# Attention halves added from PSUM, the last keys' low parts behind the first maxima, half of a scaling on ScalarE

## The chip, the cores and the metric

The kernel runs on one core of a Trainium2 chip (trn2), one launch per execution. The metric is the device time of an execution in microseconds. A profiled execution also has a span, from its first to its last instruction. The engines are TensorE (PE, with its weight loads as PEld), VectorE (DVE), ScalarE (ACT), GpSimd (POOL) and SyncE (SP, which issues the DMAs).

## The reference

One layer of a residual block over 1024 tokens of width 1024, in float32:

```python
h = rmsnorm(x, norm_mix)
proj = h @ w_in                          # 3384 columns, split between two groups of heads
o_a = sparse_attention(qa, ka, va, ...)  # 8 heads of 64; an indexer keeps 256 keys per query
o_b = gla(qb, kb, vb, ...)               # 4 heads, a recurrence over 16 chunks of 64 tokens
x = x + concat(o_a, o_b) @ w_out
h = rmsnorm(x, norm_ffn)
x = x + (silu(h @ w_ffn_gate) * (h @ w_ffn_up)) @ w_ffn_down   # width 2816
return rmsnorm(x, norm_final)
```

The attention's softmax runs over the kept keys of chunks that are not in the query's future, with a bias by relative position. The change touches three places: the copy of the projected keys, the end of the attention's product with the values, and the multiplication of the normed tokens by norm_ffn.

## The kernel before, in words

**Two parts of a number.** Matmuls run in a rounded format (fp32r). Operands are therefore split into a high part, a rounded copy made by ACT, and a low part, the difference made by DVE or POOL, and a product is the sum of three matmuls (high x high, high x low, low x high). Every operand costs an ACT copy and a subtraction.

**The order is planned.** The program does not write its instructions in a fixed order. Generators (threads) ask for an engine with a price in ns (`yield DVE, dve(256)`), for a slot of a pool, or for an event, and the class `Flow` runs them against a clock of its own; at each step it emits the instruction that could start first by its prices, and of those within 20 ns the one with the lower rank. What comes out is a fixed sequence for each engine. An event has no counterpart on the chip: it only sets where an instruction comes in its engine's sequence. Slots stand for memory: `ps` four PSUM banks of 512 columns, `pl` two double banks, `hp` seven half pages, `kb` six quarter tiles, `pg` pages. `give` returns a slot, at the planner's time.

**The keys (L1240 to 1259).** The last projection writes the keys, 128 rows (two heads) by 512 tokens to a bank. `evac_ka(hf, c, b)` copies each head's 64 rows to the high half of the key tile on ACT (L1251), writes the low part to the other 64 rows on DVE (L1257), and returns the bank. `c` is the pair of heads, 0 to 3, `hf` the half of the tokens; for c = 3 both banks are complete at the end of the projection.

**The attention.** Tokens are taken in pairs of tiles p (256 tokens), in the order 1, 2, 3, 0, and in each pair 8 heads. `softmax(p, h, e)` writes the logits lg of one tile e to a double bank (pair 0: to a ps bank), DVE adds the mask and takes the row's extreme value mn (L1337; pair 0: L1339), ACT takes the exponential (L1343), DVE a reciprocal (L1345), POOL scales (L1347), and the event ("p", t, h) is set. `value(n, i)` transposes the probabilities on PE (L1360) to a ps bank ptr, splits them (L1372 ACT, L1375 DVE) and multiplies them by the values (L1384), whose stationary operand holds high and low parts side by side: rows 0 to 63 of the output bank `av` get the products with the high parts, rows 64 to 127 those with the low parts. Two heads share an output bank. `combine(n)` adds the two halves after each second head: ACT copies the bank to a half page (L1399), the bank is returned, a quarter tile is asked for, DVE adds rows 64 to 127 to rows 0 to 63 for either head (L1405), POOL splits the sum (L1411, L1413), and SP stores it. In pair 0 the probabilities are kept in quarter tiles as well. Behind pair 3 the output projection (`oa`, L372 to 374) is open to PE as its weights arrive and are split (L257, L262).

**The second norm.** `second_norm(j, b)` adds the residual (y, L1554 for the last tile, L1567 for the others), norms the tile, transposes it on PE to banks of four blocks (tp, L1589), and `scale_tile(j, t, d0, b)` multiplies each block by norm_ffn on its way to the tile hr (L1605), two blocks at a time, with t = 1 for the tiles 0 to 3 (the last four to be made) and 0 for the others. `sum_tile` builds sums of blocks on DVE (L1663, 1667, 1671), `blocks` further differences (L1687), and `split_b` splits each into hc (L1635 ACT, L1629 DVE). The FFN multiplies by a scheme with seven products of such sums: fa, fc and fb are its first output banks, B22 (fc) is made of the t = 1 tiles, and T2 (fb) of the sums.

Of the kernel before, what the change touches and what calls it, by code (L numbers as in the profile page):

```python
# [14 lines left out]
AF = mybir.ActivationFunctionType  # L15
# [25 lines left out]
PAIRS = [1, 2, 3, 0]  # L41
# [6 lines left out]
def f32(ap):  # L48
    return ap.bitcast(F32)


PE, ACT, DVE, POOL, DMA = range(5)


def act(n, acc=False):
    return n / 1.2 + (280 if acc else 50)


def dve(n):
    return n / 0.96 + 68  # L60


def pool1(n):
    return n * 0.836 + 160


def pool2(n):
    return n * 2.105 + 150
# [6 lines left out]
def dvf(n):  # L75
    return n / 0.96 + 155
# [249 lines left out]
def block_kernel(ctx: ExitStack, tc: tile.TileContext, a: dict, out: bass.AP, dbg=None):  # L326
    nc = tc.nc
# [16 lines left out]
    def page(shape, dt, name):  # L344
        return big.tile(shape, dt, name=name, tag="pg", bufs=NPG)
# [10 lines left out]
    def half(shape, dt, name):  # L356
        return sm.tile(shape, dt, name=name, tag="hp", bufs=NHP)

    def quarter(shape, dt, name):
        return sm.tile(shape, dt, name=name, tag="kb", bufs=NKB)  # L360
# [56 lines left out]
    nrm = cst.tile([P, 2, KT], F32, name="nrm")  # L417
# [50 lines left out]
    ev = fl.event  # L468
    pg = Slots(fl, NPG - NT - 1)
    hp, kb, ps, pl = (Slots(fl, n) for n in (NHP, NKB, 4, 2))  # L470
# [768 lines left out]
    def evac_ka(hf, c, b):  # L1239
        o = slice(hf * HB, (hf + 1) * HB)  # L1240
        if hf == 0:
            yield ev("gla")
            for e in range(2):
                yield pg
                Ks[2 * c + e] = page([P, S], F32R, "K")
            ev("ka page", c).set()
        yield ev("ka page", c)
        yield ACT, 2 * act(HB)
        for e in range(2):
            r = slice(e * 64, e * 64 + 64)  # L1250
            nc.scalar.activation(Ks[2 * c + e][r, o], b[r, :], AF.Copy)  # L1251
        yield DVE, 2 * dve(HB)
        for e in range(2):
            k = Ks[2 * c + e]
            r = slice(e * 64, e * 64 + 64)
            q = slice(64 - e * 64, 128 - e * 64)
            nc.vector.scalar_tensor_tensor(k[q, o], b[r, :], 1.0, f32(k[r, o]), op0=ALU.mult, op1=ALU.subtract)  # L1257
        ps.give()
        ev("ka", hf, c).set()
# [49 lines left out]
    PB, OP = {}, {}  # L1309
# [82 lines left out]
    def combine(n):  # L1392
        p, h = units[n]
        c = h // 2
        yield ev("av", n, p)
        yield hp
        yield ACT, act(HB)
        lo = half([P, HB], F32, "lo")
        nc.scalar.activation(lo, OP.pop((p, c)), AF.Copy)  # L1399
        ps.give()  # L1400
        yield kb
        so = quarter([P, 256], F32, "so")
        for e in range(2):
            yield DVE, dve(256)
            nc.vector.tensor_tensor(so[e * 64:(e + 1) * 64, :], lo[0:64, e * 256:(e + 1) * 256],  # L1405
                                    lo[64:128, e * 256:(e + 1) * 256], op=ALU.add)
        hp.give()
        yield hp
        yield POOL, pool1(256)
        m = half([P, 2, 256], F32R, "mxa")  # L1410
        nc.gpsimd.tensor_scalar(m[:, 0, :], so, 1.0, 1.0, op0=ALU.mult, op1=ALU.mult)  # L1411
        yield POOL, pool2(256)
        nc.gpsimd.tensor_tensor(m[:, 1, :], so, f32(m[:, 0, :]), op=ALU.subtract)  # L1413
        kb.give()
        yield DMA, 450
        nc.sync.dma_start(d_ma[p][:, :, c, :], f32(m))
        hp.give(LOAD)
        ev("mix", p, c).set(LOAD)
# [122 lines left out]
    hr, BC = {}, {}  # L1541
# [57 lines left out]
    def scale_tile(j, t, d0, b):  # L1599
        o = slice(j % 4 * P, (j % 4 + 1) * P)  # L1600
        b3 = b.rearrange("p (d n) -> p d n", n=P)
        for d in range(0, 4, 2):
            yield DVE, dvf(256)
            g = nrm[:, 1, d0 + d:d0 + d + 2]
            nc.vector.tensor_tensor(hr[(d0 + d) // 2, t][:, :, o], b3[:, d:d + 2, :],  # L1605
                                    g[:, :, None].to_broadcast([P, 2, P]), op=ALU.mult)
        ps.give()
        ev("scaled", j, d0).set()
        if t and d0:
            done_b[0] += 1  # L1610
            if done_b[0] == 4:
                for k in range(4):
                    fl.spawn(split_b("B22", k, block(1, 1, k)), 1.1 + 0.01 * k)
        if bool(d0) != bool(t):
            yield ev("scaled", j, 4 - d0)
            fl.spawn(sum_tile(j) if t else first_half(j), 1.05)

    def block(j, t, k):

        return hr[2 * j + k // 2, t][:, k % 2, :]  # L1620
# [10 lines left out]
    def split_b(name, k, src):  # L1631
        yield pg
        yield ACT, acf(HB)
        w = page([P, 2, HB], F32R, "hc")
        nc.scalar.activation(w[:, 0, :], src, AF.Copy)  # L1635
        yield from low(w[:, 1, :], src, f32(w[:, 0, :]), False)
        BC[name, k] = w
        ev("B", name, k).set()
# [632 lines left out]
    def main():  # L2271
# [18 lines left out]
        yield from proj_t(evac_va)  # L2290
        yield from proj_f(evac_qa, 1)
        yield from proj_f(evac_ka, 0)
        fl.spawn(load_attention(), 15)
        fl.spawn(softmaxes(), 16)
# [62 lines left out]
```

## Time and profile before

| | us |
|---|---|
| median of 3 runs (lowest, highest) | 1287.97 (1284.92, 1291.63) |
| the profiled execution | 1289.89 |
| its span | 1288.1 |
| PE busy | 1243.2 (97% of the span) |
| DVE busy | 933.7 (72%) |
| ACT busy | 600.6 (47%) |
| POOL busy | 394.5 (31%) |

The mean granted clock of PE is 0.985 of its full speed. A share of busy time is an average over stages: the projections run to 404 us with the indexer and the recurrence beside them, the attention to about 555 us, the output projection and the second norm to about 640 us, the FFN to the end. Matmuls are pipelined and their ends are modelled, so a busy PE is not PE at its peak.

### The profile page before, as it was taken

What the parts mean: (1) busy time and instruction counts of PE and PEld (TensorE: products, weight loads), DVE (VectorE), ACT (ScalarE), POOL (GpSimd) and SP (SyncE); (2) the same over time, 40 slices, a digit from 0 to 9 for tenths busy, and PEclk for the clock granted to TensorE, in tenths of its full rate; (3) what the DMA queues carried; (4) which work ended last, traced back from release to release, by engine and by line L of the source; (5) the groups of instructions that cost most, each with busy time, mean ns of one, the idle gap of its engine ahead of it and who ended that gap; (6) DMA issues with size and microseconds to landing.
All of it is one profiled execution on the core that took longest, in us unless ns stands there. A gap on an engine that the chain in (4) does not pass through costs nothing. (4 is left out here: it accounts for less than half of the span.)

```text
span 1288.1 us, 17923 instructions
## 1 busy us (share of the span) xinstructions
PE 1243.2 (97%) x6074; PEld 1022.6 (79%) x6074; DVE 933.7 (72%) x1739; ACT 600.6 (47%) x1113; POOL 394.5 (31%) x375
## 2 busy tenths in 40 slices
PE   6999999999999999899989999999999999999997
PEld 5878878767787998778868787878888888888885
DVE  6389988979964998843688887768778653335875
ACT  4467777634524787621344444444444332222333
POOL 5324335523401544310103334334333120000340
PEclk8999999979999999999989999999999999999999
DMA  6653221334563437683015777767665479555664
GB/s 212 191 150 123 74 74 42 131 138 152 178 221 100 114 85 201 190 270 129 34 61 184 273 245 258 254 246 261 229 219 205 133 258 379 180 196 190 225 238 164
DMA packets 124909, 232.06 MB, mean 180 GB/s; under 512 B 14297, under 2 KB 72465, under 8 KB 124817
## 3 DMA queue, kind: packets, MB, share of 16 engines
q1 hardware_dynamic: 124816, 230.91, 54.4%
q8 instruction: 48, 0.79, 0.3%
q14 instruction: 45, 0.36, 0.1%
HBM read 148.02 MB, written 82.85 MB: 179 GB/s over the span
## 5 line engine op out<-in xcount | busy, mean ns | idle before, releaser
L1626 POOL TENSOR_TENSOR w<-raw,w 128x512 fp32r<-128x512 f32 x60 | 85.3, 1424 | 214.2 <-ACT w L1766 182.3
L1766 ACT ACTIVATE w<-raw 128x512 fp32r<-128x512 f32 x132 | 81.4, 626 | 54.3 <-DMA d_wd<-wd 15.0
L760 DVE TENSOR_SCALAR_CACHE_REDUCE junk_v<-acc,thr 128x768 bf16<-128x768 f32 (+3 forms) x128 | 103.7, 810 | 2.0
L262 POOL TENSOR_TENSOR w<-st,w 128x512 fp32r<-128x512 f32 x52 | 73.4, 1422 | 75.5 <-ACT w L257 73.3
L767 ACT ACTIVATE junk_a<-acc,thr 128x1024 bf16<-128x1024 f32 x64 | 73.4, 1146 | 46.2 <-DVE thr L784 37.5
L2102 DVE TENSOR_TENSOR da<-U,da 128x512 fp32r<-128x512 f32 x54 | 43.1, 799 | 53.7 <-ACT da L2100 53.5
L2100 ACT ACTIVATE da<-U 128x512 fp32r<-128x512 f32 x54 | 33.7, 630 | 98.8 <-PE da L2156 33.2
L372 PE MATMUL pj<-w,hT 128*128 128x512 f32 x192 | 79.2, 412 | 0.0
L2031 ACT ACTIVATE wd<-wd 128x512 fp32r<-128x512 f32 x77 | 48.3, 629 | 62.1 <-DMA d_wd<-wd 28.1
L373 PE MATMUL pj<-w,hT 128*128 128x512 f32 x192 | 75.9, 395 | 0.0
L374 PE MATMUL pj<-w,hT 128*128 128x512 f32 x192 | 75.8, 395 | 0.0
L372 PE MATMUL pf<-hT,w 128*128 128x512 f32 x192 | 75.8, 395 | 0.0
L1347 POOL TENSOR_SCALAR pb<-pb,sume 128x384 f32<-128x384 f32 (+3 forms) x64 | 47.7, 751 | 89.9 <-DVE sume L1345 74.1
L374 PE MATMUL pf<-hT,w 128*128 128x512 f32 x192 | 74.8, 389 | 0.0
L373 PE MATMUL pf<-hT,w 128*128 128x512 f32 x192 | 74.8, 389 | 0.0
L1807 PE MATMUL fb<-hc,w 128*128 128x512 f32 x176 | 69.5, 395 | 3.9 <-DVE gt L1842 2.5
L1808 PE MATMUL fb<-hc,w 128*128 128x512 f32 x176 | 69.2, 393 | 3.8 <-DVE hc L1629 3.8
L1808 PE MATMUL fc<-hc,w 128*128 128x512 f32 x176 | 69.5, 395 | 2.4 <-DVE hc L1629 2.4
L1807 PE MATMUL fc<-hc,w 128*128 128x512 f32 x176 | 69.1, 392 | 0.4 <-DVE gt L1861 0.4
L2156 PE MATMUL da<-db,da 128*128 128x512 f32 x176 | 68.7, 390 | 0.7 <-DVE da L2102 0.7
L1626 POOL TENSOR_TENSOR wd<-wd 128x512 fp32r<-128x512 f32 x33 | 49.8, 1511 | 63.7 <-ACT wd L2031 55.9
L2154 PE MATMUL da<-db,da 128*128 128x512 f32 x176 | 68.6, 390 | 0.6 <-ACT da L2100 0.6
(315 smaller groups left out, 3643.7 us busy)
## 6 DMA issues: line engine op xcount, KB each, us to landing
d_wd<-wd SPq DMA_DIRECT2D x77, 512.0 KB, 3.5
db<-d_wd SPq DMA_DIRECT2D x77, 512.0 KB, 4.3
st<-w_in SPq DMA_DIRECT2D x52, 256.0 KB, 2.8
raw<-w_ffn_gate SPq DMA_DIRECT2D x22, 512.0 KB, 5.2
raw<-w_ffn_up SPq DMA_DIRECT2D x22, 512.0 KB, 4.5
wd<-w_ffn_down SPq DMA_DIRECT2D x44, 256.0 KB, 4.8
d_ux<-gt SPq DMA_DIRECT2D x9, 512.0 KB, 2.6
d_uy<-gt SPq DMA_DIRECT2D x9, 512.0 KB, 3.5
```

Source lines behind the costliest of these rows:

```text
L262: (eng or self.nc.gpsimd).tensor_tensor(w[:, 1, :], st, f32(w[:, 0, :]), op=ALU.subtract)
L372: mm(ps, lh, rh, start=first, stop=False)
L373: mm(ps, lh, rl, start=False, stop=False)
L374: mm(ps, ll, rh, start=False, stop=last)
L760: v.tensor_scalar(junk_v[:, :w], acc[ts[i]], col, float(S - TOPK), op0=ALU.is_ge, op1=ALU.subtract, accum_out=cnt[:, i:i + 1])
L767: nc.scalar.activation(junk_a[:, :NA[t]], acc[t], AF.Sign, bias=thf[:, nv:], scale=-1.0, accum_out=cnt[:, nv:])
L1626: nc.gpsimd.tensor_tensor(dst, src, high, op=ALU.subtract)
L1766: nc.scalar.activation(w4[:, 0], src, AF.Copy)
L1807: mm(b, w[:, 0, kk], h[:, 0, :], start=first, stop=False, skip_group_check=True)
L1808: mm(b, w[:, 0, kk], h[:, 1, :], start=False, stop=False, skip_group_check=True)
L2154: mm(bs[t], l[:, 0, tt], r[:, 0, :], start=first, stop=False, skip_group_check=True)
L2156: mm(bs[t], l[:, 1, tt], r[:, 0, :], start=False, stop=last, skip_group_check=True)
```

## The change

The low parts of the keys for c = 3 get an event ahead of them, that of the probabilities of head 1 of the second tile of pair 1 (`PAIRS[0]` is 1). `combine` copies only rows 64 to 127 of the bank, adds rows 0 to 63 straight from PSUM, and returns the bank behind the additions; the planner's price of an addition is 362 ns where it was 335. In `scale_tile`, for t = 1, blocks 2 and 3 of each bank are scaled by ACT, one block to an instruction, with the scale read per partition.

```diff
@@ evac_ka
             nc.scalar.activation(Ks[2 * c + e][r, o], b[r, :], AF.Copy)
+        if c == 3:
+            yield ev("p", 2 * PAIRS[0] + 1, 1)
         yield DVE, 2 * dve(HB)
@@ combine
         lo = half([P, HB], F32, "lo")
-        nc.scalar.activation(lo, OP.pop((p, c)), AF.Copy)
-        ps.give()
+        b = OP.pop((p, c))
+        nc.scalar.activation(lo[64:128, :], b[64:128, :], AF.Copy)
         yield kb
         so = quarter([P, 256], F32, "so")
         for e in range(2):
-            yield DVE, dve(256)
-            nc.vector.tensor_tensor(so[e * 64:(e + 1) * 64, :], lo[0:64, e * 256:(e + 1) * 256],
+            yield DVE, dvf(256) - 60
+            nc.vector.tensor_tensor(so[e * 64:(e + 1) * 64, :], b[0:64, e * 256:(e + 1) * 256],
                                     lo[64:128, e * 256:(e + 1) * 256], op=ALU.add)
+        ps.give()
         hp.give()
@@ scale_tile
         for d in range(0, 4, 2):
+            if t and d:
+                yield ACT, 500
+                for i in (d, d + 1):
+                    nc.scalar.activation(hr[(d0 + d) // 2, t][:, i - d, o], b3[:, i, :], AF.Copy,
+                                         scale=nrm[:, 1, d0 + i:d0 + i + 1])
+                continue
             yield DVE, dvf(256)
```

## Rows read from the trace of the kernel before

**Rows 1.** The page's first part: busy us of each engine, share, instructions.
```profile
PE 1243.2 (97%) x6074; PEld 1022.6 (79%) x6074; DVE 933.7 (72%) x1739; ACT 600.6 (47%) x1113; POOL 394.5 (31%) x375
```

**Rows 2.** Stretches: us, busy us (instructions) by engine, PE's clock, DMA share, GB/s.
```profile
404.00:440.00 36.00, 32.60 (x233) 30.53 (x232) 31.09 (x98) 28.55 (x76) 16.83 (x26) 0.95 0.43 111
...
500.00:556.00 56.00, 51.15 (x325) 44.19 (x324) 43.62 (x125) 35.53 (x97) 20.76 (x34) 0.97 0.63 185
...
622.00:665.00 43.00, 36.76 (x162) 29.26 (x161) 36.28 (x76) 17.82 (x33) 3.12 (x5) 0.92 0.05 20
665.00:1288.00 623.00, 610.36 (x2681) 501.98 (x2679) 429.25 (x587) 232.09 (x398) 168.12 (x125) 1.00 0.65 227
```

**Rows 3.** PE's waits, whole span: us in total, times, longest us.
```profile
PE fb L1808 <- DVE hc L1629: 3.8, 1, 3.8
PE lg L1324 <- DVE mn L1337: 3.1, 2, 2.9
...
PE fc L1808 <- DVE hc L1629: 2.4, 1, 2.4
```

**Rows 4.** Timeline, start of the attention: start us, us, engine, line, operation, count.
```profile
405.17 2.79 DVE L1257 SCALAR_TENSOR_TENSOR K<-pf,K 64x512 fp32r<-64x512 f32 x4
...
408.25 0.69 DVE L1337 CUSTOM_DVE_ANT_0 pb<-lg,acc 128x512 f32<-128x512 f32 x1
...
410.06 1.70 PE L1360 MATMUL ptr<-mats,pb 128*128 128x128 f32 x7
```

**Rows 5.** Instructions by shape, 404 to 560 us; the last from 0 to 60.
```profile
L1405 DVE TENSOR_TENSOR so<-lo 64x256 f32<-64x256 f32 x32 | 14.9, 467 | 4.7 <-ACT lo L1399 3.9
...
L1375 DVE TENSOR_TENSOR pt<-ptr,pt 128x256 fp32r<-128x256 f32 x24 | 10.0, 419 | 3.0 <-ACT pt L1372 2.9
...
L1399 ACT ACTIVATE lo<-av 128x512 f32<-128x512 f32 x16 | 9.5, 594 | 4.5 <-PE av L1384 4.5
...
L1372 ACT ACTIVATE pt<-ptr 128x128 fp32r<-128x128 f32 x24 | 6.7, 280 | 0.0
...
L1251 ACT ACTIVATE K<-pf 64x512 fp32r<-64x512 f32 x4 | 2.4, 593 | 0.1
...
L496 ACT ACTIVATE hT<-tp,nrm 128x512 fp32r<-128x512 f32 x16 | 9.7, 694 | 3.2 <-PE tp L522 3.2
```

**Rows 6.** Timeline: the copy and the second addition of two units.
```profile
430.30 0.60 ACT L1399 ACTIVATE lo<-av 128x512 f32<-128x512 f32 x1
...
432.42 0.42 DVE L1405 TENSOR_TENSOR so<-lo 64x256 f32<-64x256 f32 x1
...
522.02 0.60 ACT L1399 ACTIVATE lo<-av 128x512 f32<-128x512 f32 x1
...
536.12 0.45 DVE L1405 TENSOR_TENSOR so<-lo 64x256 f32<-64x256 f32 x1
```

**Rows 7.** Timeline around the longest addition.
```profile
487.13 1.02 POOL L1347 TENSOR_SCALAR pb<-pb,sume 128x896 f32<-128x896 f32 x1 [0.23 <-DVE sume L1345]
487.28 1.13 DVE L1405 TENSOR_TENSOR so<-lo 64x256 f32<-64x256 f32 x1 [0.32 <-ACT lo L1399]
```

**Rows 8.** Timeline, second norm and first products; in brackets idle time before and its end.
```profile
627.40 2.19 DVE L1605 TENSOR_TENSOR hr<-tp,nrm 128x256 f32<-128x256 f32 x6 [1.80 <-PE tp L1589]
...
630.10 1.52 DVE L1605 TENSOR_TENSOR hr<-tp,nrm 128x256 f32<-128x256 f32 x4 [0.52 <-PE tp L1589]
...
635.56 0.68 DVE L1554 TENSOR_TENSOR y<-oa,y 128x512 f32<-128x512 f32 x1
...
635.77 0.60 ACT L1834 ACTIVATE gt<-fa 128x512 f32<-128x512 f32 x1 [9.36 <-PE fa L1809]
...
646.75 0.68 DVE L1629 TENSOR_TENSOR hc<-hr,hc 128x512 fp32r<-128x512 f32 x1
...
652.14 0.69 DVE L1849 TENSOR_TENSOR gt<-fc,gt 128x512 f32<-128x512 f32 x1 [1.90 <-PE fc L1809]
...
658.40 0.68 DVE L1629 TENSOR_TENSOR hc<-hr,hc 128x512 fp32r<-128x512 f32 x1
```

## The prediction

> **What bounds the kernel now.** I read the page's busy times first: TensorE (PE) is busy 1243.2 of 1288.1 us [rows 1], so a gain has to come out of its 44.9 us of idle time, or out of time at its lower clock. The table of stretches comes second, because the change moves nothing before 404 us, where the last key columns are evacuated. The four stretches shown of what follows hold 36 - 32.60 = 3.4, 56 - 51.15 = 4.85, 43 - 36.76 = 6.2 and 623 - 610.36 = 12.6 us of idle PE [rows 2]. Third, PE's waits: the three longest behind 404 us, 3.8, 2.9 and 2.4 us, all end with VectorE (DVE) [rows 3]. Two stand at 644 to 660 us (fc and fb, the first products of the FFN, wait for the low part hc), one at 406 us (the logits lg wait for a row maximum mn). Behind each PE ran at its lower level, 1.2 instead of 2.4 GHz: 404 to 440 us has a granted clock of 0.95, which costs 0.05 x 36 = 1.8 us, and 622 to 665 us has 0.92, so 0.08 x 43 = 3.4 us for its two drops [rows 2]. What the change can reach directly is therefore 2.9 + 1.8 at 406 us and 2.4 + 3.8 + 3.4 at 644 us, 14.3 us in all. The sum below is made against the profiled execution, 1289.89 us (its span of 1288.10 and 1.79 around it); the median of the runs, 1287.97, is 1.92 below it.
>
> **One thing beneath all three edits.** The order on each engine comes from the planner's prices, events and slots. A bank that is given back later, or a DVE price of 362 ns instead of 335, can reorder everything behind it. I allow 2 us either way for that, from the PE idle of the two stretches that are named by no edit, 4.85 and 12.6 us [rows 2].
>
> **Edit 1, low parts of the last keys.** Four DVE instructions, 2.79 us together, stand at 405.17 [rows 4]. Directly behind them, at 408.25, comes the maximum of the fourth tile, and PE waits 2.9 us for it [rows 3, 4]. The new event puts the four behind the finished probabilities of that tile. Taken out, the maximum starts at about 405.2, and the wait and its drop of the clock go: 2.9 + 1.8 = 4.7 us at best. The four do not vanish. ScalarE (ACT) has the key copies first, then three exponentials of 0.7 to 0.9 us; by these I estimate the probabilities ready near 409.6, so the 2.79 us come at about 409.7 to 412.5, just where the first transposed probabilities want DVE. What is late next is bank space: both PSUM banks of the key columns, two of four, stay taken until then instead of 408, and one of the other two is the output bank. The transposes, seven in one go at 410.06 now [rows 4], must run as four, then a copy (0.6) and a low part (0.7), both of 512 columns, then three. If the 2.79 us come ahead of that low part, the second group ends near 413.7 instead of 411.4: 2.3 us worse, and with the clock's 1.8 a loss of 4.1. So the bounds are a gain of 4.7 and a loss of 4.1. DVE's work is the same in both orders and PE's next work is limited by it, so I take a value well below the best: a gain of 1.5 us.
>
> **Edit 2, halves added from PSUM.** ACT's copy shrinks from 128 to 64 partitions with the same 512 columns. The key copies of 64 x 512 take 593 ns, the present copy 594 [rows 5]: nothing is saved, 16 times. The 32 additions read one half from PSUM. DVE's nearest form with a PSUM operand, 128x256, has a mean of 419 ns, the present additions 467 [rows 5], one that nothing disturbs 0.42 us [rows 6]. So DVE gets up to 32 x 47 ns = 1.5 us back; at the other end it loses what the planner's two prices differ by, 32 x 27 ns = 0.9 us.
> The longest addition, 1.13 us, starts inside a GpSimd instruction and ends after it [rows 7]. The Trainium skill (SBUF — State Buffer, "Who interferes with whom") says that a DVE instruction with two SBUF inputs and a GpSimd instruction that reads SBUF shut each other out, and one with a single SBUF input does not; by that the 1.5 us come back whole. The Trainium skill (Perfetto Trace Analysis, "Optimizing Scalar/DVE Operations") speaks against the edit: about 125 ns of access for DVE on PSUM against 60 on SBUF, an estimate of 32 x 65 ns = 2.1 us more DVE time and, if PE waited for all of it, a sum 2.1 us higher; the 419 ns do not bear that out.
> The real price is the bank. It was free when ACT's copy ended; now it is free when the second addition ends. That is 432.84 instead of 430.90 in an ordinary unit, 1.9 us, but 536.57 instead of 522.62 for the last unit of pair 3 [rows 6]: that combine waits for a quarter tile (kb), and these are held by the probabilities of pair 0. One or two of four banks blocked there starve transposes and logits. Cover: the output projection stands ready as PE's filling, as far as its weights are split. Without that cover the price is at most the 14 us of that hold; with it, a quarter of the 16 ordinary holds (16 x 1.9 / 4 = 7.6 us) is already far, and the other end is the 1.5 us of DVE as a gain. I take a loss of 1.0 us, near the cheap end, because softmaxes short of a bank also stop taking kb, which hands kb to the combine sooner.
>
> **Edit 3, half of a scaling on ACT.** Of the 16 instructions of 128x256 for the four tiles t = 1, 8 leave DVE. They follow each other at (2.19 - 0.42) / 5 = 0.354 us when six stand together [rows 8], so 2.8 us. 16 instructions of 128x128 come to ACT: 280 ns each by the copy of that shape, plus 100 ns for a scale read per partition (694 against 594 at 512 columns) [rows 5], so 280 to 380 ns each. ACT had been idle for 9.4 us at 635.77 [rows 8], beside the first twelve of them, so these cost nothing. Five of the eight (three of six at 627.40, two of four at 630.10) stand ahead of y at 635.56, which waits in DVE's order and not for PE [rows 8]: y, the last tile's norm and its transposes come 1.8 us sooner. With one more of the last tile's halves gone, hc of 646.75 [rows 8], for which fc waits, comes about 2.1 us sooner: the wait of 2.4 nearly goes, with its clock 2.1 + 1.7 = 3.8 us. Late next is T2: PE comes to fb 3.8 us sooner, while its hc of 658.40 gains 2.1, the 1.9 us that DVE waited for PE at 652.14 [rows 8], and 0.35 for one more half: 4.3 us. So the second wait and its drop stay, and the stretch ends 4.3 us sooner. Against that nearly all of ACT's 17.8 us of this stretch [rows 2] lie behind 635.77, splits of weights and of hc that the planner ranks higher, and the last tile's four ACT halves come between them: two of 0.3 to 0.4 us on the chain, 0.8 us. I take a gain of 3.5 us. Bounds: both waits and both drops gone, 2.4 + 3.8 + 3.4 = 9.6; or the ACT halves queued behind all of the splits (4 x 0.38 = 1.5, nothing gained), a loss of 1.5.
>
> **Sum.** -1.5 + 1.0 - 3.5 = -4.0 us: 1289.89 - 4.0 = 1285.9 for a profiled execution, and 1287.97 - 4.0 = 1284.0 for the median. Almost all of it must arrive, since PE is busy 610 of the last 623 us [rows 2].
>
> **Rivals.**
> *More goes than I take.* Both starts lose their waits and drops: 4.7 and 7 of the 9.6, -11.7: 1276.3. For it: each drop of the clock costs as much as a wait and vanishes whole. Against it: DVE stays over 84% busy in both places (36.28 of 43, 31.09 of 36) [rows 2], so some wait returns.
> *Nothing that can be seen.* The starts gain and the transition from pair 3 to pair 0 gives it back, by banks or by another order: 1288. For it: PE's 4.85 us there [rows 2] come from the same resources that edit 2 holds longer.
> *Slower: banks.* One mechanism: a bank that waits for DVE. The 2.79 us fall ahead of the first low parts (+4.1), and in the transition the combines hold banks until kb comes, of which the filling covers half of 14 us (+7); edit 3's 3.5 us are kept: +7.6, 1295.6. It decides where the second group of transposes, or the output bank of pair 0, is asked for before the additions ahead of it have run. For it: the 13.9 us hold. Against: without a bank the planner has other PE work at 520 to 550 us.
> *The edit does not do what it says:* the halves on ACT come in behind the splits and B22 waits for ACT instead of DVE; edit 3 is then 0 and the sum -0.5, 1287.5, counted with the second rival.
>
> **How the numbers follow.** Forecast 0.42, more 0.22, nothing 0.20, slower 0.16. Under 0.5% (6.4 us, about what a measurement of this kernel can tell from no change) lies between 1281.5 and 1294.4. Faster: the 0.22 and 0.09 of the forecast, whose own range is 1280 to 1288: 0.31. Slower: 0.12 of the last rival and 0.01 of the third. Same: 0.56. The range reaches to the second rival's centre, and to the fourth's short of its price: 1275.5 to 1292.5.
>
> **What would show it.** Edit 1: the four K instructions behind the fourth maximum, lg without a wait of 2.9 us, the clock of 404 to 440 us above 0.95. Edit 2: additions with a mean near 420 ns, and PE's idle in 500 to 556 us near 5 us; 10 or more is the slower rival. Edit 3: y near 633.8 before any shift, fc's wait under 0.5 us, fb's still 3 us or more. I am wrong on the mechanism if PE's idle from 622 to 665 us, shifted as the stage shifts, stays at 6 us, or if the idle behind 665 us moves by more than 3.

## The result, and the profile after

The change made the kernel slower: 1293.87 us against 1284.36 us for the kernel before (medians of 17 runs each on the same chips), a ratio of 1.0063 with an interval of 1.0046 to 1.0081, +8.1 us. The forecast had a gain of 4.0 us, and 1293.87 lies above its range, even though the 17 runs put the kernel before 3.6 us below the three that the prediction started from. The profiled execution has a span of 1292.1 us.

The page's first part, answering [rows 1]: PE's work is the same, DVE's is not lower, and ACT has 9 us more.

```profile
PE 1242.1 (96%) x6074; PEld 1020.7 (79%) x6074; DVE 935.9 (72%) x1731; ACT 609.7 (47%) x1129; POOL 394.1 (31%) x375
```

The stretches of [rows 2] in the changed kernel (columns as there):

```profile
404.00:440.00 36.00, 31.65 (x233) 29.03 (x232) 31.79 (x98) 28.11 (x75) 18.29 (x28) 1.00 0.41 109
500.00:556.00 56.00, 48.17 (x292) 41.19 (x291) 39.44 (x119) 33.04 (x90) 18.66 (x32) 0.91 0.58 175
622.00:665.00 43.00, 37.30 (x172) 29.88 (x172) 32.85 (x66) 22.88 (x50) 3.18 (x5) 0.96 0.06 25
```

The second row is the loss: PE idle 56 - 48.17 = 7.8 us where it was 4.85, at a clock of 0.91 where it was 0.97. Fixed windows mislead a little here, since the stages shift. The next two views therefore count from the first logits (lg), which start at 401.8 us before and 399.1 after; the 2.7 us between them lie in a part that no edit touches. First the kernel before, 0 to 20, 20 to 60, 60 to 100 us behind the first logits, and from there to the first product of the FFN (fa), then the same of the changed kernel:

```profile
401.80:421.80 20.00, 17.06 (x109) 15.60 (x108) 15.91 (x50) 14.78 (x39) 7.25 (x12) 0.91 0.56 141
421.80:461.80 40.00, 39.50 (x308) 37.83 (x307) 36.26 (x105) 31.27 (x78) 21.38 (x31) 1.00 0.48 122
461.80:501.80 40.00, 39.26 (x285) 35.89 (x284) 37.37 (x87) 32.00 (x70) 19.03 (x21) 1.00 0.42 113
501.80:632.90 131.10, 126.01 (x678) 106.13 (x677) 73.06 (x178) 48.50 (x120) 26.79 (x48) 0.99 0.54 171
```

```profile
399.10:419.10 20.00, 16.65 (x113) 14.73 (x112) 16.16 (x52) 14.56 (x39) 7.16 (x12) 1.00 0.63 157
419.10:459.10 40.00, 38.26 (x289) 35.56 (x288) 35.02 (x99) 31.82 (x76) 20.79 (x30) 1.00 0.44 113
459.10:499.10 40.00, 39.72 (x295) 37.02 (x293) 36.61 (x87) 33.46 (x69) 18.85 (x21) 1.00 0.41 111
499.10:638.30 139.20, 130.42 (x680) 108.84 (x681) 73.44 (x178) 53.97 (x134) 27.57 (x49) 0.96 0.50 162
```

From the first logits to the first fa it is 231.1 us before and 239.2 after: +8.1 us, and nearly all of it in the last row, which is 8.1 us longer for the same count of matmuls (678 and 680). PE idles 8.8 us of it instead of 5.1. The granted clock is at 0.5 for 10.2 us of it instead of 3.4; half of PE's busy time in these stretches is 4.1 us instead of 1.5, so the clock costs 2.6 us more. Together that is 6.3 of the 8.1 us; the rest lies in PE's busy time, whose ends are modelled, and is not placed. From the first fa to the end the changed kernel needs 653.8 us instead of 655.2.

**The start.** The timeline around the keys' low parts, to be held against [rows 4]:

```profile
404.08 0.27 PE L1362 MATMUL ptr<-mats,pb 128*128 128x128 f32 x1
...
405.55 0.88 PE L1362 MATMUL ptr<-mats,pb 128*128 128x128 f32 x6 [1.20 <-POOL pb L1349]
...
406.57 2.81 DVE L1259 SCALAR_TENSOR_TENSOR K<-pf,K 64x512 fp32r<-64x512 f32 x4
...
409.41 1.22 DVE L1377 TENSOR_TENSOR pt<-ptr,pt 128x512 fp32r<-128x512 f32 x3
...
410.16 0.63 PE L1386 MATMUL av<-pt,V 128*128 128x256 f32 x3 [1.74 <-DVE pt L1377]
```

The transposes begin 5.0 us behind the first logits (404.08) instead of 8.3, and the wait of 2.9 us for a maximum [rows 3] is gone. But the four low parts now stand in front of the first low parts of probabilities (409.41), and PE waits 1.2 and 1.74 us that it did not wait before. The first copy of two heads' values (`lo`) comes 16.3 us behind the first logits; before it was 16.2.

**The additions.** Shapes, answering [rows 5]:

```profile
L1407 DVE TENSOR_TENSOR so<-av,lo 64x256 f32<-64x256 f32 x32 | 13.4, 418 | 7.9 <-ACT lo L1402 5.5 <-PE ptr L1362 1.5
...
L1402 ACT ACTIVATE lo<-av 64x512 f32<-64x512 f32 x16 | 9.5, 594 | 6.7 <-PE av L1386 6.3
```

They fell from 467 to 418 ns, and the copy of half the partitions costs the same 594 ns. The Trainium skill (SBUF — State Buffer, "Who interferes with whom") has it so: with one SBUF input the addition is no longer shut out by GpSimd. The Trainium skill (Perfetto Trace Analysis, "Optimizing Scalar/DVE Operations") has about 125 ns of access on PSUM against 60 on SBUF, an estimate of 65 ns more for an operand in PSUM. That is not seen: 418 ns stand against 0.42 us for an undisturbed addition from SBUF [rows 6]. The 1.5 us of DVE came back, and bought nothing that can be seen: sbuf_order below, with the old additions in the same order, is as slow.

**From pair 3 to pair 0.** The copies and additions of three combines, answering [rows 6], and the copy of the first combine of pair 0. The bank is now taken until the second addition:

```profile
427.77 0.59 ACT L1402 ACTIVATE lo<-av 64x512 f32<-64x512 f32 x1
...
429.63 0.42 DVE L1407 TENSOR_TENSOR so<-av,lo 64x256 f32<-64x256 f32 x1
...
512.12 0.59 ACT L1402 ACTIVATE lo<-av 64x512 f32<-64x512 f32 x1
...
521.34 0.59 ACT L1402 ACTIVATE lo<-av 64x512 f32<-64x512 f32 x1 [0.74 <-PE av L1386]
...
523.84 0.42 DVE L1407 TENSOR_TENSOR so<-av,lo 64x256 f32<-64x256 f32 x1
...
531.90 0.42 DVE L1407 TENSOR_TENSOR so<-av,lo 64x256 f32<-64x256 f32 x1
...
533.48 0.59 ACT L1402 ACTIVATE lo<-av 64x512 f32<-64x512 f32 x1 [0.42 <-PE av L1386]
```

An ordinary bank is held 2.3 us (427.77 to 430.05), the last two of pair 3 are held 12.1 and 11.0 us. The first combine of pair 0 (533.48), the 13th of 16, comes 134.4 us behind the first logits and 12.1 us behind the last of pair 3. In the kernel before it comes 123.9 us behind the first logits and 3.7 us behind the last of pair 3, whose copy stands at 522.02 [rows 6]:

```profile
525.71 0.60 ACT L1399 ACTIVATE lo<-av 128x512 f32<-128x512 f32 x1
```

Then SP's queue in the changed kernel, and DVE and PE 9 us later:

```profile
535.40 0.42 SPq L1498 DMA_DIRECT2D y<-x  x1
535.87 0.42 SPq L1500 DMA_DIRECT2D mxb<-d_mb  x1
536.61 0.57 SPq L1501 DMA_DIRECT2D mxa<-d_ma  x1
537.97 5.75 SPq L1419 DMA_DIRECT2D d_ma<-mxa  x2
```

```profile
546.90 0.62 DVE L1377 TENSOR_TENSOR ptl<-ptr,pth 128x256 fp32r<-128x256 f32 x2 [4.16 <-DMA d_ma<-mxa]
...
547.38 0.58 PE L1386 MATMUL av<-ptl,V 128*128 128x256 f32 x1 [3.85 <-DVE ptl L1377]
```

A low part of pair 0 is to be written to a half page whose content is still being stored: that store was issued behind three loads of 512 KB for the next tile and landed 8.8 us later. PE waits 3.85 us, and from the 146th to the 157th us behind the first logits its granted clock is 0.5 (1.2 GHz).

**The FFN's start.** PE's waits over the whole span, answering [rows 3]:

```profile
PE av L1386 <- DVE ptl L1377: 4.4, 2, 3.9
PE fb L1817 <- DVE hc L1638: 3.8, 1, 3.8
...
PE fc L1816 <- ACT hc L1644: 1.1, 1, 1.1
...
PE fc L1817 <- DVE hc L1638: 0.8, 1, 0.8
```

Then the first 36 us from the first fa, cut at the first fb, before and after (columns as in [rows 2]):

```profile
632.90:654.80 21.90, 19.48 (x81) 15.11 (x79) 17.97 (x40) 9.56 (x18) 1.17 (x2) 0.92 0.06 25
654.80:668.90 14.10, 10.28 (x39) 8.06 (x39) 13.53 (x24) 9.44 (x17) 0.00 (x0) 0.88 0.00 0
```

```profile
638.30:658.20 19.90, 18.01 (x82) 14.12 (x81) 16.33 (x35) 10.96 (x22) 1.24 (x2) 1.00 0.07 27
658.20:674.30 16.10, 12.29 (x41) 9.51 (x41) 14.10 (x25) 9.50 (x17) 0.00 (x0) 0.79 0.00 0
```

fc's wait of 2.4 us has become 1.1 and 0.8, and the clock stayed up behind both (1.00 where it was 0.92): from fa to fb it is 19.9 us instead of 21.9. fb's wait is 3.8 us as before, but the clock behind it is lower for longer, 0.79 instead of 0.88: it is at 0.5 for 6.8 us instead of 3.4. The 0.96 of the stretch 622 to 665 us above is therefore no gain: the stretch ends before that drop does.

Most of the 2.0 us between fa and fb is not edit 3's. Four kernels below keep the scaling of the kernel before and its wait of 2.4 us for fc, and the clock stays up behind that wait all the same (price, nudge_copy, inplace, psum_hp8). In price, fa to fb (columns as in [rows 2]):

```profile
631.60:652.00 20.40, 17.98 (x81) 13.96 (x79) 18.04 (x40) 9.56 (x18) 1.17 (x2) 1.00 0.07 27
```

Where no drop stands behind fc, edit 3 has 19.9 us for 20.4. And y came no sooner, as DVE's timeline in the changed kernel shows against [rows 8]:

```profile
643.36 0.68 DVE L1557 TENSOR_TENSOR y<-oa,y 128x512 f32<-128x512 f32 x1
...
651.93 2.49 DVE L1638 TENSOR_TENSOR hc<-hr,hc 128x512 fp32r<-128x512 f32 x4
```

y stands 5.0 us behind the first fa instead of 2.7, behind more sums of blocks and a split of w than before. The hc for which fc waits begins 13.6 us behind the first fa instead of 13.9.

### The profile page after: what moved, and what is told of

Its sections match the earlier page's. It is cut to its first block, busy times and chain, and to the rows that moved or that the text cites. A ratio compares the mean times of both kernels' runs of the same rounds, so it can differ in the third digit from the quotient of the medians.

```text
span 1292.1 us, 17953 instructions
## 1 busy us (share of the span) xinstructions
PE 1242.1 (96%) x6074; PEld 1020.7 (79%) x6074; DVE 935.9 (72%) x1731; ACT 609.7 (47%) x1129; POOL 394.1 (31%) x375
## 5 line engine op out<-in xcount | busy, mean ns | idle before, releaser
L1817 PE MATMUL fb<-hc,w 128*128 128x512 f32 x176 | 69.9, 397 | 3.8 <-DVE hc L1638 3.8
L1816 PE MATMUL fb<-hc,w 128*128 128x512 f32 x176 | 69.9, 397 | 2.2 <-DVE gt L1851 1.5
L1818 PE MATMUL fb<-hc,w 128*128 128x512 f32 x176 | 69.7, 396 | 0.0
```

The costliest lines, as they stand in the source:

```text
L1816: mm(b, w[:, 0, kk], h[:, 0, :], start=first, stop=False, skip_group_check=True)
L1817: mm(b, w[:, 0, kk], h[:, 1, :], start=False, stop=False, skip_group_check=True)
L1818: mm(b, w[:, 1, kk], h[:, 0, :], start=False, stop=k == 3, skip_group_check=True)
```

## The experiments

Ratios to the kernel before, with intervals; each kernel was compared on one chip in five rounds. "lg to fa" is the time from the first logits to the first fa in the one profiled execution. In it, "idle" is what PE's busy time leaves of it, and "clock" the sum over windows of 1 us of busy time x (1 - granted clock). Both can be off by about 1 us, since matmul ends are modelled.

| kernel | ratio | lg to fa | idle | clock |
|---|---|---|---|---|
| before | 1 | 231.1 | 9.2 | 3.2 |
| the change | 1.0063 [1.0046, 1.0081] | 239.2 | 14.1 | 4.1 |
| keys: edit 1 alone | 1.0045 [1.0027, 1.0064] | 236.9 | 12.3 | 5.0 |
| psum: edit 2 alone | 1.0064 [1.0039, 1.009] | 238.3 | 13.5 | 4.7 |
| scale: edit 3 alone | 0.9983 [0.9966, 1.0] | 230.2 | 9.5 | 1.7 |
| keys_scale: edits 1, 3 | 1.0043 [1.0026, 1.0061] | 236.0 | 12.5 | 3.4 |
| sbuf_order | 1.0068 [1.005, 1.0085] | 237.5 | 13.1 | 4.4 |
| hold | 1.0066 [1.0049, 1.0083] | 239.3 | 14.8 | 4.9 |
| hold_123 | 1.0054 [1.0033, 1.0075] | 237.7 | 15.0 | 3.4 |
| psum_hp8 | 1.0042 [1.0022, 1.0061] | 236.9 | 11.5 | 5.0 |
| inplace | 1.0027 [1.0012, 1.0042] | 232.7 | 9.5 | 3.4 |
| keys_late | 1.0074 [1.0054, 1.0093] | 236.2 | 12.8 | 3.4 |
| keys_free | 1.0037 [1.0017, 1.0057] | 236.9 | 12.4 | 3.2 |
| price | 1.0025 [1.0001, 1.0048] | 232.7 | 10.2 | 3.3 |
| nudge_down | 1.0056 [1.0037, 1.0075] | 234.5 | 11.9 | 3.3 |
| nudge_copy | 1.0041 [1.0026, 1.0056] | 234.1 | 11.6 | 3.4 |
| scale_recip | 1.005 [1.0031, 1.0069] | 237.5 | 13.0 | 4.9 |
| scale_pool | 0.9987 [0.997, 1.0004] | 230.5 | 8.9 | 3.3 |
| scale_hp8 | 0.9988 [0.9972, 1.0005] | 230.2 | 9.7 | 1.7 |
| inplace_scale | 1.002 [1.0003, 1.0037] | 232.7 | 9.4 | 3.4 |

**The edits one by one** (each the part of the diff that bears its name).

keys: 

> Edit 1 alone: the low parts of the last keys behind the first maxima. Banks theory (the loss comes from output banks held until the additions, edit 2): faster than before by 1 to 3 us, PE's wait of 2.9 us at the first logits gone, pair 0 as long as before. Store theory (the loss is one wait of DVE for a half page whose store lands late, an accident of the order that any earlier edit can bring): the time follows whether that wait of 4 us stands in this trace, +5 to +8 us with it, -1 to -3 without. Keys theory (the four low parts, now in the middle of the first units, starve them): slower by 2 to 4 us, with PE idle 406 to 412 us.

psum: 

> Edit 2 alone: the halves added straight from PSUM, the bank given back behind the additions. Banks theory: slower by 5 to 9 us, the attention from the first logits to the last product with the values 6 us or more longer than before. Store theory: slower only if DVE waits some 4 us for a store in pair 0; otherwise within 2 us of before. Keys theory: no loss, within 2 us, additions of 417 ns instead of 467.

scale: 

> Edit 3 alone: half of the scaling on ScalarE for the last four tiles. All theories: faster by 1 to 3.5 us, the attention as before to within 0.5 us, the wait at the first fc product under 1 us, that at fb still 3 to 4 us.

keys_scale: 

> Edits 1 and 3 together, edit 2 undone. Banks theory: faster than before by 2 to 6 us. Store theory: as keys plus scale, so slower if the wait for the store stands in keys. Keys theory: within 2 us of before.

Edits 1 and 2 each lose, 5.8 and 8.2 us of 1285, and not in sum: together with edit 3 they lose 8.1. In psum the bank theory came true; the store theory's wait stands there too (3.9 us of DVE). keys has no wait of 4 us for a store, and its loss is above the 2 to 4 us of the keys theory. keys_scale, at a loss of 5.5 us, lies outside what the banks and the keys theory allowed and has no such wait either. Edits 2 and 3 were not run together.

Edit 3 gains 2.2 us by its median, but its interval ends at 1.0. scale_hp8 and scale_pool below, which hold it too, are at 0.9988 and 0.9987; by the medians it is worth 0.0002 on top of edit 1 and 0.0007 on top of inplace below. In scale its wait for fc was 1.1 and 0.8 us, not under 1 us in all.

**Where edit 2 loses: the operand, the bank or the price.** sbuf_order keeps edit 2's sequence on every engine, with the old copy and the old operands; hold keeps the old price too; price changes nothing but the price:

```diff
@@ sbuf_order (hold: the same with dve(256))
-        nc.scalar.activation(lo, OP.pop((p, c)), AF.Copy)
-        ps.give()
+        b = OP.pop((p, c))
+        nc.scalar.activation(lo, b, AF.Copy)
...
-            yield DVE, dve(256)
+            yield DVE, dvf(256) - 60
...
+        ps.give()
@@ price
-            yield DVE, dve(256)
+            yield DVE, dvf(256) - 60
```

> Edit 2's order with the old instructions: all 128 rows copied to SBUF, both additions from SBUF, but the bank counted as held until the second addition and the addition at its new planner price, so that the products, transposes, loads and stores of all engines come in the same order as in the kernel with edit 2 alone (1.0064 of before). Order theory (edit 2 loses by the order that the planner writes once a bank is held longer, not by where the addition reads): as slow as edit 2 alone, 1.006 +-0.0025 of before, the 13th copy of a pair of heads again about 134 us after the first logits (before 123.9), and a store wait of about 4 us in pair 0. Operand theory (the additions from PSUM cost the time on the chip): within 0.002 of before, and the store wait below 2 us. Additions again at a mean of 460 to 470 ns in either case.

> The kernel before with one thing changed: the bank of a pair's values is counted as held until the second addition (old price, old instructions). Bank theory: 1.004 to 1.007 of before, first copy of pair 0 at 130 to 135 us after the first logits (before 123.9). Price theory (the planner's 27 ns higher price of an addition is what shifts the order): within 0.002 of before.

> The kernel before with only the planner's price of an addition raised by 27 ns (the banks given back as before, same instructions): no instruction costs more, the order alone shifts. Bank theory: within 0.002 of before (1283 to 1287 us). Price theory: 1.004 to 1.007. If it comes out anywhere beyond 0.002 to either side, a nudge of the order by itself is worth that much, and the two units of the prediction's allowance for reordering were too small.

sbuf_order is as slow as edit 2 (1.0068), hold as well (1.0066). So the operand is not the cause; that the planner counts the bank as taken for longer is enough. The first combine of pair 0 comes 134.7 and 135.9 us behind the first logits, as in edit 2 (134.6). Some details missed: hold's 135.9 lies beyond its 130 to 135, the store's wait was 2.5 and 2.3 us, not 4, and the additions from SBUF had a mean of 490 ns, not 460 to 470. price, which changes no instruction, loses 0.0025 as well. That is beyond what it was allowed, though its interval nearly reaches 1, and it opened the question of the order.

**Which bank.** hold_123 holds it only in the first three pairs (`ps.give()` stays at its old place where p is 0).

> The kernel before with the bank held until the second addition in the first three pairs alone, and given back after the copy, as before, in pair 0. Transition theory (the last combines of the third pair keep banks from pair 0's first units): first copy of pair 0 again about 134 us after the first logits, 1.004 to 1.007 of before. Pair 0 theory (the loss of pair 0 is made by its own held banks): first copy of pair 0 at 124 to 128 us, 1.001 to 1.003, the 2.7 us of pairs 1 to 3 alone.

1.0054, with pair 0's first combine at 135.8 us: it is not pair 0's own banks, but those of the pairs ahead of it, that put pair 0 back, as the transition theory has it. Most of it comes at the end of pair 3: the last copy of pair 3 is 3.4 us later than before, the next one, the first of pair 0, 11.9 us.

**The store.** psum_hp8 gives edit 2 an eighth half page that the planner does not count. The sequences stay, and each half page is written again one turn later.

```diff
-        return sm.tile(shape, dt, name=name, tag="hp", bufs=NHP)
+        return sm.tile(shape, dt, name=name, tag="hp", bufs=NHP + 1)
```

> Edit 2 alone with one more half page behind the pool of seven: the planner still counts seven, so the order of all instructions is that of edit 2 alone (1.0064), but each half page is used again one turn later, so that a low part of pair 0 no longer waits for a store queued behind the next tile's loads. Store theory (that wait, 3.9 us of DVE and 3.6 of TensorE, with the halved clock behind it, 3.0 us, is most of edit 2's loss): 1.000 to 1.003 of before, no clock of 0.5 after the 100th us of the attention. Pure order theory (the postponed pair 0 leaves TensorE short of work whatever the store does; the wait only covers it): 1.005 to 1.007.

The waits of PE from 495 to 560 us in psum_hp8, where edit 2 alone has 4.1 us for the low part of pair 0:

```profile
PE oa L373 <- DVE w L262: 2.3, 3, 1.3
...
PE av L1384 <- DVE ptl L1375: 0.5, 1, 0.5
```

The wait is gone and 1.0064 has become 1.0042: by the medians the store was a third of the loss, between the two theories. The intervals overlap widely, and from the first logits to fa it is 1.4 us less. The clock still falls to 0.5 there, for 3.3 us of loss. By itself, in scale_hp8, the eighth half page gives nothing: 0.9988, where 0.997 to 0.9985 and the fastest of all were expected.

> Edit 3 alone with the eighth half page behind the pool: instructions and their order are those of edit 3 alone (0.9983). Store theory: ScalarE's wait of 1.3 us for a store in pair 0 goes; TensorE waits there at most 0.4 us for it, so 0.997 to 0.9985 of before; it is to be the fastest of all. If it is slower than edit 3 alone by over 0.001, the moved addresses cost something that no theory here has.

**The quarter tile.** inplace writes the sum into the half page of the copy, so that no quarter tile is asked for between copy and additions:

```diff
-        yield kb
-        so = quarter([P, 256], F32, "so")
+        so = lo[:, 0:256]
...
-        hp.give()
         yield hp
...
-        kb.give()
+        hp.give()
```

> Edit 2 alone, with the sum written into the half page that holds the copy (its first 64 rows are free since only 128 rows' lower half is copied, and the second addition may overwrite what the first has read), so that no quarter page is waited for between copy and additions; seven half pages as before. Quarter theory (the bank is held long because the additions wait for a quarter page while pair 0's probabilities hold them): the longest stretch from a copy to its second addition falls from 10 to 12 us to under 6, the first copy of pair 0 comes at 122 to 130 us after the first logits, and the time is 0.998 to 1.003 of before. Hold theory (any time longer in the bank, even 1.5 us, pushes the order): 1.004 to 1.007.

Its last two combines of pair 3 and the first of pair 0, copy and additions:

```profile
510.80 0.59 ACT L1400 ACTIVATE lo<-av 64x512 f32<-64x512 f32 x1
511.53 0.87 DVE L1404 TENSOR_TENSOR lo<-av,lo 64x256 f32<-64x256 f32 x2
...
519.41 0.59 ACT L1400 ACTIVATE lo<-av 64x512 f32<-64x512 f32 x1
...
522.62 0.42 DVE L1404 TENSOR_TENSOR lo<-av,lo 64x256 f32<-64x256 f32 x1
...
523.55 0.59 ACT L1400 ACTIVATE lo<-av 64x512 f32<-64x512 f32 x1
...
528.79 0.42 DVE L1404 TENSOR_TENSOR lo<-av,lo 64x256 f32<-64x256 f32 x1
```

The two of pair 3 hold their banks 1.6 and 3.6 us instead of 12.1 and 11.0, the first of pair 0 comes at 126.0 us and holds 5.7, no store is waited for, and the time is 1.0027. So by the medians 0.0037 of edit 2's 0.0064 goes with the wait for a quarter tile. The store's wait goes with it; and since the order differs as well, a part of it may be the order's.

**Edit 1: the collision or the bank.** keys_late waits for a later event (head 3 instead of 1). keys_free copies the keys' bank to SBUF, gives it back at once, and makes the late low parts from the copy:

```diff
@@ keys_free, ahead of the low parts
+        if c == 3:
+            yield hp
+            yield ACT, act(HB)
+            s = half([P, HB], F32, "kc")
+            nc.scalar.activation(s, b, AF.Copy)
+            ps.give()
+            b = s
+            yield ev("p", 2 * PAIRS[0] + 1, 1)
```

> Edit 1 alone with a later event: the last keys' low parts wait for the probabilities of the fourth head instead of the second, so that DVE works off the first low parts of probabilities ahead of them; the keys' bank is held longer for it. Collision theory (edit 1 loses since the four low parts, 2.81 us, stand in front of the first low parts of probabilities, which stops TensorE for 1.7 us and halves its clock behind it for 1.6 us): 1.000 to 1.003 of before against 1.0045 for edit 1, no clock of 0.5 in the first 20 us. Bank theory of edit 1 (the keys' bank, kept longer, is what is missing): 1.0045 or more.

> Edit 1 alone, but the last keys' bank is first copied to SBUF by ScalarE (one more copy of 128x512, about 0.6 us) and given back at once; the low parts then read the copy, after the same event. Bank theory of edit 1 (the loss is the bank that waits with the low parts): 0.998 to 1.001 of before, the first transposes again 5 us after the first logits, the fourth copy of the values no later than before (36.1). Collision theory (four low parts in front of the first low parts of probabilities): 1.003 to 1.006, as edit 1 alone.

Neither theory holds for both. keys_late moved the low parts out of the way and got slower, 1.0074, with 5.2 us of idle PE in the first 20 us, as the bank theory had it. keys_free freed the bank and stayed at 1.0037, with the fourth copy at 37.8 us, later than before, as the collision theory had it. In edit 1 alone the first four copies come at most 1.5 us later than before; from the eighth on (76.1 us against 71.3) it is about 5 us late. There PE, then DVE, show this:

```profile
474.31 1.41 PE L1362 MATMUL ptr<-mats,pb 128*128 128x128 f32 x11
477.62 1.52 PE L1386 MATMUL av<-pt,V 128*128 128x256 f32 x4 [1.89 <-DVE pt L1377]
```

```profile
475.15 1.59 DVE L1407 TENSOR_TENSOR so<-lo 64x256 f32<-64x256 f32 x2 [0.32 <-ACT lo L1401]
476.78 1.89 DVE L1377 TENSOR_TENSOR pt<-ptr,pt 128x512 fp32r<-128x512 f32 x3
```

Eleven transposes in one go, then PE waits for the low parts behind two additions, 1.89 us, and runs at 0.5 of its clock for 3.4 us. It is 70 us behind the moved instructions. The kernel before has no such wait at this place (0.7 us of idle in those 40 us, in the third row of its table above), and neither has the whole change (0.3 us).

**The order itself.** So I shifted the order with nothing else: the planner's price of an addition 27 ns lower (nudge_down), of the copy 30 ns higher (nudge_copy), and on top of edit 3 the reciprocal's 25 ns higher (scale_recip) and GpSimd's scaling 30 ns lower (scale_pool). Every instruction stays.

```diff
@@ nudge_down
-            yield DVE, dve(256)
+            yield DVE, dve(256) - 27
@@ nudge_copy
-        yield ACT, act(HB)
+        yield ACT, act(HB) + 30
@@ scale_recip
-        yield DVE, 75
+        yield DVE, 100
@@ scale_pool
-        yield POOL, pool1(n) + 80
+        yield POOL, pool1(n) + 50
```

> The kernel before with the planner's price of an addition lowered by 27 ns, every instruction the same: only the order shifts. Picked-order theory (the order of before is one of the best that this planner writes, so any shift of it loses, whichever its sign): 1.001 to 1.005, as the raised price (1.0025). Random theory (a shift is as likely to gain): anywhere from 0.996 to 1.004, and the mean over the three nudges of prices (up, down, the copy's) within 0.001 of 1.

> The kernel before with the planner's price of the values' copy raised by 30 ns, every instruction the same. Picked-order theory: 1.001 to 1.005. Random theory: 0.996 to 1.004, with the mean over the three nudges of prices within 0.001 of 1.

> Edit 3 alone (0.9983 of before) with the planner's price of the attention's reciprocal at 100 ns for 75, every instruction the same: a shift of the order at another place than the three nudges before, which all stood in the combine. Picked-order theory: 0.9993 to 1.004 of before, slower than edit 3 alone by 0.001 to 0.0055. Combine theory (only shifts around the combine lose, since they move banks): within 0.001 of edit 3 alone.

> Edit 3 alone with the planner's price of GpSimd's scaling of the probabilities lower by 30 ns, every instruction the same. Picked-order theory: 0.9993 to 1.004 of before. Combine theory: 0.997 to 0.999, and where it is under 0.9975 it is the best version here.

PE's timeline in nudge_copy, then in scale_recip:

```profile
471.50 1.61 PE L1360 MATMUL ptr<-mats,pb 128*128 128x128 f32 x11
475.00 0.35 PE L1384 MATMUL av<-pt,V 128*128 128x256 f32 x1 [1.89 <-DVE pt L1375]
```

```profile
479.56 1.62 PE L1360 MATMUL ptr<-mats,pb 128*128 128x128 f32 x11
483.06 1.38 PE L1384 MATMUL av<-pt,V 128*128 128x256 f32 x4 [1.89 <-DVE pt L1375]
```

It is the stall of edit 1, to the hundredth of a microsecond, some 75 us behind the first logits, in kernels that touch no key. keys_free, nudge_down and keys_scale have it as well. These six are at 1.0037 to 1.0056; against edit 3 alone, scale_recip loses 1.005 / 0.9983 = 1.0067. Idle PE from 60 to 100 us is 2.5 to 2.6 us in these kernels where it is 0.7 before, and in four of them the clock takes some 1.7 us more; the rest of their loss is spread. Two nudges go free of the stall: price loses 0.0025 and scale_pool nothing (0.9987). So no strict theory holds: not every shift loses, those that do are not only in the combine, and the mean of the three nudges of the kernel before is 1.0041, not within 0.001 of 1. Four of five lose, none gains.

A shifted order can thus lose as much as the held bank, and the size of a loss does not tell one from the other. The place does. From the last copy of pair 3 to the first of pair 0 it is 12.1 to 12.2 us in all six kernels that hold the bank there until the additions and wait for a quarter tile (the change, psum, sbuf_order, hold, hold_123, psum_hp8), 3.6 to 3.7 us in the kernel before and in all five nudges, and 4.1 us in inplace. None of the six has the stall.

**Together.** 

> Edit 2 with the sum in the copy's half page (1.0027 of before) and edit 3 (0.9983) together. If the two add up, 1.001 +-0.002 of before; the waits of fc below 1.2 us and that of fb near 3.8, as in edit 3 alone. If the saved additions only pay once edit 3 has freed ScalarE and DVE behind them, 0.997 to 0.999.

1.002, within its interval the sum of the two. Edit 3 alone has the lowest ratio of all versions, 0.9983 (1283.5 us); with an interval that ends at 1.0 the gain is not sure.

## Why the prediction was wrong, point by point

Two terms of the sum failed: edit 2's, which holds the larger part, and the allowance for the order.

**The allowance for the order** was "2 us either way". It was taken from the idle PE of the kernel before, as if a new order could only move what idles. A new order makes idle time that was not there: price, nudge_down and nudge_copy, with not one instruction changed, cost 3.2, 7.2 and 5.3 us (the ratio's excess over 1, times 1285). It was also two-sided, and all nudges were on one side or zero. With this term at a loss of some 4 us the sum would have been near zero, and still 8 us short. The stall of the nudges is not in the changed kernel; what its new order costs stands at the transition, under edit 2.

**Edit 1** (a gain of 1.5, bounds a gain of 4.7 and a loss of 4.1; measured a loss of 5.8). The first half was right: the maximum comes 3.0 us sooner and the wait of 2.9 us goes. So was the collision that stood at the other bound: the low parts ahead of the first low parts of probabilities, PE waiting 1.74 us. Start to start the two cancel: the first copy comes 1.5 us later in edit 1 alone and 0.1 us later in the whole change. What the prediction did not have is the stall 70 us on, which belongs to the order and not to the keys, since nudges show it. The changed kernel has the collision but not the stall, and its first 100 us hold no more of idle PE and lost clock than before (5.4 us against 5.9), so little of what edit 1 loses alone can be in its +8.1 us. What else edit 1 alone loses is open: freeing the bank changed 1.0045 to 1.0037, inside the intervals, and keeping it longer brought 1.0074.

**Edit 2** (a loss of 1.0, bounds a gain of 1.5 and a loss of 14; measured a loss of 8.2). The mechanism, a bank held while the combine waits for a quarter tile, was named, with its place, and is shown: holding alone reproduces the loss, and taking the quarter tile's wait away returns 0.0037 of it, 4.8 us. The step that failed is the size, "near the cheap end": the cover by the output projection, and the quarter tiles that were to come sooner. These did come sooner, but not by enough: the additions of pair 3's last combine end 11.0 us behind its copy, where it was 14.5 [rows 6], and the first copy of pair 0 is put back by 10.5 us. The projection's matmuls did fill PE while pair 0 was put back: 48 of them run by the 140th us behind the first logits in either kernel. In the next 10 us the changed kernel runs none, the kernel before 15; there PE waits and its clock falls. It comes to 3.7 us of idle and 2.6 of clock more, by the last rows of the two tables from the first logits. The store behind 1.5 MB of loads was in no step; a landing that the planner prices at 2.5 us took 8.8. The forecast of DVE's side was right (418 ns, no cost of PSUM as an operand).

**Edit 3** (a gain of 3.5; measured 2.2). Right in sign and near in size, but not by its steps. fc's wait was to fall under 0.5 us and is 1.9 in two parts, one of them for ACT (the halves and splits there, priced at 0.8). The chain to it failed at y: y was to come 1.8 us sooner and came 2.3 us later, and hc, forecast 2.1 us sooner, came 0.3 sooner, since three more sums of blocks, a split of w and DVE's wait for it (0.9 us) now stand ahead of y. The drop of the clock behind fc's wait is gone, but it is gone in four kernels without edit 3 too; the prediction had tied a drop to each wait. By the prediction's own test, the idle time of this stage, the mechanism is hardly there: 36 us from the first fa hold 5.7 us of idle PE, before 6.2. This 0.5 us is all of the gain that the traces place. That the attention is 0.9 us shorter in scale's trace is no work of the edit: each engine's order is there the one of the kernel before, whose clock falls to 0.5 for 3.4 us at 144 us behind the first logits; in scale it does not.

**The rivals.** The slower one, 1295.6 for +7.6 by banks, was nearly the result, +8.1, and its sign of recognition, 10 us of idle in 500 to 556, came half as idle (7.8) and half as clock (0.91). It had 0.16. It had the place and the mechanism of the transition, but its sum was in part luck: of its +4.1 at the start nothing came, and edit 3 alone measured 2.2, not 3.5. That planning alone, with no instruction changed, could lose was in none; the second rival only let another order give a gain back.

## What to carry to other kernels

Where a planner writes the order, an edit's own gain stands against the change of the whole sequence behind it. Measure that by itself, with a price nudged by some 30 ns that changes no instruction; here, in a tuned kernel, four of five such nudges lost, by 3 to 9 us, and an edit has to be worth more than that to show. An edit that releases a scarce buffer later is priced by the longest wait that can now fall between taking and giving it, so take what the wait is for (here the quarter tile) out of that stretch first. And before a gain or a loss is put down to an edit, look for the same drop of the clock in kernels that do not have the edit: here one drop, absent in some kernels behind the very same wait, was worth 1.6 us (fa to fb, 22.0 against 20.4 us), and edit 3, by what the traces place, 0.5.

## What had not been expected of the hardware

A store of 256 KB issued behind three loads of 512 KB on the same queue took 8.8 us to land, where the median of these stores was 2.6. The granted clock fell to 0.5 in the last 1.7 us of the 3.85 us wait that it caused and stayed there for 10.2 us, of which PE was busy 8.2; behind the 1.74 us wait at 410 us it did not fall at all (1.00 from 404 to 440 us). The same wait did not always bring the same drop: behind the stall of 1.89 us the clock was at 0.5 for 3.4 us in edit 1 alone and did not fall in nudge_copy, and behind the wait of 2.4 us for fc it was at 0.5 for 3.4 us in the kernel before and did not fall in price.
